# Norm factors of the delta-rule heads: four heads in one set of instructions

## The chip, the cores and the metric

The kernel runs on one core of one Trainium2 chip. The metric is the device time of one execution in microseconds (us); lower is better. Five engines work side by side, each through a queue of its own in order: TensorE (PE in the profile; its weight loads are PEld), VectorE (DVE), ScalarE (ACT), GpSimd (POOL), and SyncE (SP), which issues the DMAs here.

## The reference, cut to what matters

One layer of a decoder is computed for 1024 prompt tokens and 32 sample tokens: an input projection, two groups of heads side by side (four gated-delta heads of width 128, and sliding-window attention), an output projection, two layer norms and a SwiGLU. The change concerns the unit-length scaling of k and q in the delta heads:

```
def l2norm(t):
    return t * lax.rsqrt(jnp.sum(t * t, axis=-1, keepdims=True) + EPS)

q = l2norm(qc.reshape(Bn, L, H_A, DK_A)) * (DK_A ** -0.5)
k = l2norm(kc.reshape(Bn, L, H_A, DK_A))
...
A = jnp.where(strict, jnp.einsum('bnhid,bnhjd->bnhij', kb, kc) * decay, 0.0)      # kb = kc * beta
rhs = jnp.concatenate([vc * bc[..., None], kb * jnp.exp(gc)[..., None]], axis=-1)
...
o_n = q_dec S + qk v_new;   S = S * g_last + k_dec^T v_new
```

## The kernel before, in words

The prompt is taken in two passes, s = 0 (columns 0 to 511) and s = 1 (512 to 1055; its last 32 columns are the sample tokens). In each, 22 tiles of the input projection are multiplied one after the other; `conv_dense`, `kv_dense`, `q_dense` and `z_dense` issue them. Each weight quarter is split into a rounded part (`wh`, ACT, L162) and a remainder (`wl`, DVE, L163), and each product is three matmuls (L433 to L435). All other work is written as generators: `spawn` puts one on a list, and `pump` runs through the list between groups of matmuls until a budget of estimated work is spent. A generator that waits for a flag yields BLOCK and is passed over. `TileContext(nc, schedule_with_timeline_sim=True)` then lays out the order within each engine's queue from its own estimates, so neighbouring generators are interleaved.

The k and q of a head are not scaled by their norms; the scale is carried as factors, kept in the small tile `hs[s]` with fields of 4 x 4 columns (head x block of 128 tokens). In `delta_k(s, h)` ACT sums the squares of k (L668) into `ssk`; DVE adds EPS (L672), takes the reciprocal `rk2` (L673) and `wk` = rk2 times a decay (L674), and scales the block matrix `Ball` with rk2 (L678), which gives the flag K. Then it takes the reciprocal root of `ssk` in `rsqrt` (two integer instructions, L410 and L411, and three Newton steps of three instructions, L413 to L415) and from it `bsk` (L685, L686), flag B. `delta_q(s, h)` does the same for q (L806 to L816): `rq` and `rqe`, flag Q. So each head has a k chain and a q chain of 14 instructions of 128x4, each of which reads what the one before wrote.

Who reads them: `delta_v` scales v with `bsk` (L832) once B is set; `delta_w` waits for the inverse (flag E) and for Q; `recur` waits for Q, V and W of all heads and uses `wk` (L872), `rqe` (L887) and `rq` (L911, L914). `inverse(s)` waits for K of all heads and runs 31 steps of two instructions on POOL (L710, L712). At the same time DVE takes the row maxima of the attention scores (L1074, which frees the score banks in PSUM), the softmax scaling (L1096) and the convolutions (L642). `page` hands out a buffer of SBUF, and POOL clears its first column (L229) before anyone writes it; DVE's first writes of `pre` (L624, L626) wait for that.

Of the kernel before, what the change touches and what calls it, by code (L numbers as in the profile page):

```python
# [12 lines left out]
ALU = mybir.AluOpType  # L13
AX = mybir.AxisListType

P = 128
# [8 lines left out]
EPS = 1e-6  # L25
# [183 lines left out]
def _program(k):  # L209
# [3 lines left out]
    V, A, G = nc.vector, nc.scalar, nc.gpsimd  # L213
# [7 lines left out]
    def room(tag, n=1):  # L221
        return cap[tag] - live[tag] >= n
# [34 lines left out]
    def drop(tag="hp", n=1):  # L257
        live[tag] -= n
        assert live[tag] >= 0
# [13 lines left out]
    def b3(ap):  # L273

        return ap.unsqueeze(2).broadcast_to([P, 4, P])
# [6 lines left out]
    def spawn(g, quick=False):  # L282
        gens.append(g)
        if quick:
            fast.append(g)
# [17 lines left out]
    def need(cond):  # L303
        while not cond():
            assert pump(), "no progress"
# [5 lines left out]
    flags = set()  # L311

    def wait(*names):
        while not all(n in flags for n in names):
            yield BLOCK
# [92 lines left out]
    def rsqrt(x, y, a):  # L408

        V.tensor_scalar(a.bitcast(I32), x.bitcast(I32), 1, None, ALU.logical_shift_right)  # L410
        V.tensor_scalar(y.bitcast(I32), a.bitcast(I32), -1, 0x5F3759DF, ALU.mult, ALU.add)  # L411
        for _ in range(3):
            V.scalar_tensor_tensor(a, y, -0.5, y, ALU.mult, ALU.mult)  # L413
            V.tensor_tensor(a, a, x, ALU.mult)
            V.scalar_tensor_tensor(y, a, 1.5, y, ALU.add, ALU.mult)  # L415

    def groups(s):
        return [(0, 512)] if s == 0 else [(0, 272), (272, 272)]
# [53 lines left out]
    gat = {}  # L472
# [101 lines left out]
    hs = {}  # L574
# [45 lines left out]
    def conv_dense(s, ti, ft):  # L620
        need(lambda: room("hp", 2))
        pre = page([P, 3 + 512], F32, f"pre{s}{ft}")
        if s == 0:
            V.memset(pre[:, 0:3], 0.0)  # L624
        else:
            V.tensor_copy(pre[:, 0:3], carry[:, ft, :])  # L626

        def evac(ps, c0, cw):
            pw = min(512, c0 + cw) - c0
            A.copy(pre[:, 3 + c0:3 + c0 + pw], ps[:, :pw])  # L630
            if pw < cw:
                A.copy(XS[:, ft, :, 3:7], ps[:, pw:cw].rearrange("p (b t) -> p b t", t=4))

        dense(idx[f"in{s}"][TILES.index(ti)], *x_hl[s], evac, groups(s))
        return pre
# [14 lines left out]
    def delta_k(s, h, pre):  # L650

        F = hs[s]
        yield from have("hp", 2)
        kT = page([P, 512], F32, f"kT{s}{h}")
        kN = page([P, 4, P], F32, f"kN{s}{h}")
        heads[s, h] = d = {"kT": kT, "kN": kN}
        yield from conv(s, 4 + h, pre, kT)
        yield from have("ms", 2)
        pk, pb = bank(), bank()
        pk3 = pk.rearrange("p (n t) -> p n t", t=P)  # L660
        for n in range(4):
            tr(pk3[:, n, :], kT[:, n * P:(n + 1) * P], ident)
        for n in range(4):
            mm(pb[:, n * P:(n + 1) * P], kT[:, n * P:(n + 1) * P], kT[:, n * P:(n + 1) * P], start=True, stop=True)
        A.copy(kN, pk3)
        for n in range(4):
            jk = small([P, P], "junk", 1)
            A.activation(jk, pk3[:, n, :], AF.Square, accum_out=F["ssk"][:, h, n:n + 1])  # L668
        drop("ms")
        yield 1300.0  # L670
        ss, rk2, y, a = (F[n][:, h, :] for n in ("ssk", "rk2", "y", "a"))
        V.tensor_scalar(ss, ss, EPS, None, ALU.add)  # L672
        V.reciprocal(rk2, ss)  # L673
        V.tensor_tensor(F["wk"][:, h, :], rk2, gat[s]["ekd"][:, h * 4:h * 4 + 4], ALU.mult)  # L674
        yield from wait(("R", s, h))
        RB = Bm[s][:, h * 4:h * 4 + 4, :]
        for n in range(4):
            V.scalar_tensor_tensor(RB[:, n, :], pb[:, n * P:(n + 1) * P], rk2[:, n:n + 1], RB[:, n, :],  # L678
                                   ALU.mult, ALU.mult)
        drop("ms")  # L680
        flags.add(("K", s, h))
        yield 0.0
        rsqrt(ss, y, a)
        bsk = F["bsk"][:, h, :]
        V.tensor_tensor(bsk, ss, y, ALU.mult)  # L685
        V.tensor_tensor(bsk, bsk, gat[s]["beta"][:, h * 4:h * 4 + 4], ALU.mult)  # L686
        flags.add(("B", s, h))
        yield 0.0

    def inverse(s):  # L690
# [98 lines left out]
    def delta_q(s, h, pre):  # L789
        F = hs[s]  # L790
        yield from have("hp")
        qT = page([P, SG[s][1]], F32, f"mx{s}{h}")
        mixed[s, h] = qT
        yield from conv(s, h, pre, qT[:, 0:512])
        yield from wait(("R", s, h))
        yield from have("ms", 2)
        d = heads[s, h]
        R = Rt[s, h]
        pq, pb = bank(), bank()
        for n in range(4):  # L800
            tr(pq[:, n * P:(n + 1) * P], qT[:, n * P:(n + 1) * P], ident)
        for n in range(4):
            mm(pb[:, n * P:(n + 1) * P], d["kT"][:, n * P:(n + 1) * P], qT[:, n * P:(n + 1) * P], start=True, stop=True)
        for n in range(4):
            jk = small([P, P], "junk", 1)
            A.activation(jk, pq[:, n * P:(n + 1) * P], AF.Square, accum_out=F["ssq"][:, h, n:n + 1])  # L806
        for n in range(4):
            V.scalar_tensor_tensor(R[:, n, :], pb[:, n * P:(n + 1) * P], F["rk2"][:, h, n:n + 1], R[:, n, :],
                                   ALU.mult, ALU.mult)
        drop("ms", 2)  # L810
        yield 1300.0
        ss, rq, rqe, y, a = (F[n][:, h, :] for n in ("ssq", "rq", "rqe", "yq", "aq"))
        V.tensor_scalar(ss, ss, EPS, None, ALU.add)
        rsqrt(ss, y, a)
        V.tensor_scalar(rq, y, float(P) ** -0.5, None, ALU.mult)
        V.tensor_tensor(rqe, rq, gat[s]["eg"][:, h * 4:h * 4 + 4], ALU.mult)  # L816
        flags.add(("Q", s, h))
        yield 0.0

    def delta_v(s, h, pre):  # L820
        yield from have("hp", 2)
# [13 lines left out]
        yield 450.0  # L835

    def delta_w(s, h):
        yield from wait(("E", s), ("Q", s, h))
        yield from have("hp")
        d = heads[s, h]  # L840
        bE = page([P, 4, P], F32, f"bE{s}{h}")
        V.tensor_tensor(bE, Em[s][:, h * 4:h * 4 + 4, :], b3(gat[s]["bg"][:, h * 4:h * 4 + 4]), ALU.mult)
        yield 0.0
        yield from have("ms")
        pw = bank()
        for n in range(4):
            mm(pw[:, n * P:(n + 1) * P], d["kN"][:, n, :], bE[:, n, :], start=True, stop=True)
        drop()
        d["wT"] = d["kT"]
        A.activation(d["wT"], pw, AF.Copy, scale=-1.0)  # L850
        drop("ms")
        flags.add(("W", s, h))
        yield 900.0
# [3 lines left out]
    def recur(s):  # L857

        F, g = hs[s], gat[s]
        yield from wait(*[(x, s, h) for x in "QVW" for h in range(4)])  # L860
        hd = [heads[s, h] for h in range(4)]
        Eall = Em[s]
        if s:
# [1 line left out]
        for n in range(4):  # L865
# [42 lines left out]
            for h in range(4):  # L908
                o = hd[h]["vb"][:, n, :]
                rq = F["rq"][:, h, n:n + 1]  # L910
# [16 lines left out]
        v, y, a = F["oss"], F["y"], F["a"]  # L927
# [514 lines left out]
    def mix_in(s, before_last):  # L1442
        fields(s)
        pre = conv_dense(s, 0, 4)
        baT = ba_dense(s)
        if s == 0:
            params()
        spawn(gating(s, baT))
        for h in range(4):
            spawn(decay(s, h))  # L1450
        spawn(delta_k(s, 0, pre))
        for h in range(1, 4):
            spawn(delta_k(s, h, conv_dense(s, h, 4 + h)))
        spawn(inverse(s))
        spawn(keys(s, kv_dense(s, 12, "kb")))
        spawn(vals(s, kv_dense(s, 13, "vb")))
        for m in range(4):
            spawn(attn(s, m, q_dense(s, m)))
        if s:
            spawn(history())  # L1460
            spawn(sample_attn(), True)
        for h in range(4):
            spawn(delta_q(s, h, conv_dense(s, 4 + h, h)))
        for h in range(4):
            spawn(delta_v(s, h, conv_dense(s, 8 + h, 8 + h)))
            spawn(delta_w(s, h))
        spawn(recur(s))
        if s:
            spawn(sample_delta(), True)
        for h in range(3):  # L1470
            spawn(gate(s, h, z_dense(s, h)))
        hook = before_last()
        spawn(gate(s, 3, z_dense(s, 3, ktmajor=True, hook=hook)))
        if s == 0:
            spawn(spill())
        drop("xs", 8)
        hook(1)
# [179 lines left out]
    for f in range(NE):  # L1657
        q = quarters(f)
        plan[f] = {n: W.plain(W.raw(q[n])) for n in ("A11", "A12")}
    for f in range(NF):  # L1660
        q, early = quarters(f), f < NE
# [3 lines left out]
        p = plan.setdefault(f, {})  # L1665
# [36 lines left out]
    B = {}  # L1702
# [195 lines left out]
    for f in range(NF):  # L1898
        end = f == NF - 1
        p = plan[f]  # L1900
# [6 lines left out]
        q = banks("ms", HW_)  # L1907
# [13 lines left out]
        q = banks("acc", HW_)  # L1921
# [7 lines left out]
        q = banks("acc", 512)  # L1929
# [10 lines left out]
        q = banks("ms", HW_)  # L1940
# [151 lines left out]
```

## Time and profile before

| | |
|---|---|
| median of 3 runs | 1296.59 us (1295.82 to 1296.64) |
| profiled execution | 1296.37 us |
| its span, first to last instruction | 1294.6 us |
| granted TensorE clock over the span | 0.985 |
| busy: PE, PEld | 1253.7 us, 1130.8 us |
| busy: DVE, ACT, POOL | 889.3 us, 619.0 us, 396.1 us |

Times inside the profile count from the start of the span. An instruction's row gives its line in the kernel, its operation, and the tiles as out<-in; idle time in front of it stands in brackets with what ended it. The granted clock is a share of full speed: 1.00 is 2.4 GHz and 0.50 is 1.2 GHz, and a mean over a stretch lies between them.

### The profile page before, as it was taken

Reading aid. Unit: us, or ns where it says so; the run is one execution under the profiler, and the core shown is the slowest. Engines: PE = TensorE matmul, PEld = TensorE weight load, DVE = VectorE, ACT = ScalarE, POOL = GpSimd, SP = SyncE. Lnnn points to the kernel's source line nnn. Section 1 sums busy time; section 2 is a strip of 40 time slices with the busy share of each in tenths; the row PEclk is TensorE's granted clock in tenths of the full one; section 3 lists DMA queues with packets and bytes.
Section 4 is the critical chain, followed back from the end, with each engine's and each line's share of the span. In section 5 each row is a group of like instructions: output and inputs, shape, how many; then the busy total and the mean of one; then the engine's idle time right before and its main releaser. Section 6 shows DMA issues by size and latency. Waiting matters only on the chain.

```text
span 1294.6 us, 25112 instructions
## 1 busy us (share of the span) xinstructions
PE 1253.7 (97%) x8701; PEld 1130.8 (87%) x8701; DVE 889.3 (69%) x2041; ACT 619.0 (48%) x1376; POOL 396.1 (31%) x1207
## 2 busy tenths in 40 slices
PE   9998999999999999996999999999999999999996
PEld 7876789989889988985999999999999898788995
DVE  6797975888995679868866655555655775632664
ACT  7774754657656543586322222323324554522453
POOL 1008411203913134527643433222332112111210
PEclk9998999999899999998999999999999999999998
DMA  7422331242143556444544422222324886634461
GB/s 251 139 82 75 83 135 47 82 142 75 35 124 113 169 162 192 162 152 150 174 148 150 138 99 68 81 83 75 111 86 118 293 262 184 206 115 114 142 219 47
DMA packets 119103, 170.82 MB, mean 132 GB/s; under 512 B 20272, under 2 KB 50096, under 8 KB 118960
## 3 DMA queue, kind: packets, MB, share of 16 engines
q1 hardware_dynamic: 118976, 169.22, 41.7%
q8 instruction: 68, 1.11, 0.3%
q14 instruction: 59, 0.48, 0.1%
HBM read 138.44 MB, written 31.75 MB: 131 GB/s over the span
## 4 chain that ended last, share of the span: by engine, by line
PE 77%; DVE 12%; issue 3%; ACT 3%; DMA 2%; POOL 2%; DVEq 0%; SPq 0%; ACTq 0%; POOLq 0%
PE acc L1978 6%; PE acc L1807 6%; PE acc L1976 6%; PE acc L1977 6%; PE acc L1808 6%; PE acc L1809 6%; PE acc L433 5%; PE acc L434 5%; PE ms L1809 5%; PE ms L1807 5%; PE acc L435 5%; PE ms L1808 5%; DVE wl L163 2%; DVE st L1074 1%; PE ms L1123 1%
## 5 line engine op out<-in xcount | busy, mean ns | idle before, releaser
L163 DVE TENSOR_TENSOR wl<-wr,wh 128x512 fp32r<-128x512 f32 x330 | 238.6, 726 | 133.6 <-ACT wh L162 123.5
L162 ACT CAST wh<-wr 128x512 fp32r<-128x512 f32 x330 | 197.4, 602 | 264.1 <-PE acc L1977 104.9
L433 PE MATMUL acc<-xh,wh 128*128 128x272 f32 (+1 forms) x528 | 175.1, 332 | 0.2 <-DVE qs L1032 0.2
L435 PE MATMUL acc<-xh,wl 128*128 128x272 f32 (+1 forms) x528 | 173.9, 329 | 1.2 <-DVE wl L163 1.1
L434 PE MATMUL acc<-xl,wh 128*128 128x272 f32 (+1 forms) x528 | 173.6, 329 | 0.0
L1978 PE MATMUL acc<-hx,wl 128*128 128x272 f32 (+1 forms) x528 | 171.6, 325 | 1.9 <-DVE wl L163 1.8
L1976 PE MATMUL acc<-hx,wh 128*128 128x272 f32 (+1 forms) x528 | 171.9, 326 | 1.3 <-ACT wh L162 1.3
L162 ACT CAST wh<-S 128x512 fp32r<-128x512 f32 x88 | 54.4, 619 | 150.6 <-PE acc L1808 95.7
L1978 PEld LDWEIGHTS acc<-hx,wl 128*128 128x128 f32 x528 | 99.2, 188 | 11.4 <-DVE wl L163 3.2
L435 PEld LDWEIGHTS acc<-xh,wl 128*128 128x128 f32 x528 | 100.4, 190 | 9.2 <-DVE wl L163 1.8
L434 PEld LDWEIGHTS acc<-xl,wh 128*128 128x128 f32 x528 | 100.6, 190 | 8.5 <-issue 2.0
L433 PEld LDWEIGHTS acc<-xh,wh 128*128 128x128 f32 x528 | 100.5, 190 | 8.3 <-issue 1.0
L1976 PEld LDWEIGHTS acc<-hx,wh 128*128 128x128 f32 x528 | 99.1, 188 | 9.8 <-ACT wh L162 1.9
L1977 PE MATMUL acc<-hx,wh 128*128 128x272 f32 x352 | 101.4, 288 | 0.2 <-DVE hx L1706 0.2
L163 DVE TENSOR_TENSOR wl<-S,wh 128x512 fp32r<-128x512 f32 x88 | 72.1, 821 | 37.7 <-ACT wh L162 35.0
L1977 PE MATMUL acc<-hy,wh 128*128 128x512 f32 x176 | 69.2, 393 | 0.0
L1977 PEld LDWEIGHTS acc<-hx,wh 128*128 128x128 f32 x352 | 66.4, 189 | 0.7 <-DVE hx L1706 0.4
L433 PE MATMUL acc<-mh,wh 128*128 128x272 f32 (+1 forms) x192 | 64.0, 333 | 0.0
L434 PE MATMUL acc<-ml,wh 128*128 128x272 f32 (+1 forms) x192 | 63.4, 330 | 0.0
L435 PE MATMUL acc<-mh,wl 128*128 128x272 f32 (+1 forms) x192 | 63.0, 328 | 0.0
L1705 ACT CAST hx<-hr 128x272 fp32r<-128x272 f32 (+1 forms) x66 | 31.6, 485 | 47.4 <-DMA hr<-hd 43.1
L1647 POOL TENSOR_TENSOR S<-wr,S 128x512 f32<-128x512 f32 x22 | 34.7, 1577 | 54.5 <-DVE wl L163 54.5
(631 smaller groups left out, 3519.2 us busy)
## 6 DMA issues: line engine op xcount, KB each, us to landing
wr<-in_w_ffo_t SPq DMA_DIRECT2D x120, 256.0 KB, 3.0
wr<-in_w_ffi_t SPq DMA_DIRECT2D x108, 256.0 KB, 2.8
wr<-in_w_in_t SPq DMA_DIRECT2D x88, 256.0 KB, 2.8
wr<-in_w_out_t SPq DMA_DIRECT2D x32, 256.0 KB, 2.6
hd<-x SPq DMA_DIRECT2D x22, 272.0 KB, 2.5
hr<-hd SPq DMA_DIRECT2D x44, 136.0 KB, 2.7
hd<-x SPq DMA_DIRECT2D x22, 256.0 KB, 2.0
hr<-hd SPq DMA_DIRECT2D x22, 256.0 KB, 4.9
```

The costliest lines, as they stand in the source:

```text
L162: nc.scalar.copy(hi, raw)
L163: nc.vector.tensor_tensor(lo, raw, hi.bitcast(F32), ALU.subtract)
L433: mm(ps[:, :cw], wh, xh[kt][:, c0:c0 + cw], start=(kt == 0), stop=False)
L434: mm(ps[:, :cw], wh, xl[kt][:, c0:c0 + cw], start=False, stop=False)
L435: mm(ps[:, :cw], wl, xh[kt][:, c0:c0 + cw], start=False, stop=(kt == n - 1))
L1647: G.tensor_tensor(t["S2"], W.get(r["A12"]), t["S2"], ALU.subtract)
L1807: mm(o, wh[:, kt, :], xh, start=(start and kt == 0), stop=False, **kw)
L1808: mm(o, wh[:, kt, :], xl, start=False, stop=False, **kw)
L1809: mm(o, wl[:, kt, :], xh, start=False, stop=(kt == 3), **kw)
L1976: mm(ps, wh[:, f % 4, :], xh, start=(f == 0), stop=False)
L1977: mm(ps, wh[:, f % 4, :], xl, start=False, stop=False)
L1978: mm(ps, wl[:, f % 4, :], xh, start=False, stop=(f == NF - 1))
```

## The change

The k chain after the flag K, with `wk`, moves out of `delta_k` into a new generator `norms_k(s)`; the q chain moves out of `delta_q` into `norms_q(s)`. Each waits for all four heads and then works on the fields of all of them, 128x16 in place of 128x4. `norms_k` is spawned after the four `delta_k`, `norms_q` after the four `delta_q`. `delta_q` now sets a flag q as soon as its block matrix is scaled, for which `delta_w` waits; `recur` waits for one flag Q of the pass.

```
     def delta_k(s, h, pre):
...
-        ss, rk2, y, a = (F[n][:, h, :] for n in ("ssk", "rk2", "y", "a"))
+        ss, rk2 = (F[n][:, h, :] for n in ("ssk", "rk2"))
         V.tensor_scalar(ss, ss, EPS, None, ALU.add)
         V.reciprocal(rk2, ss)
-        V.tensor_tensor(F["wk"][:, h, :], rk2, gat[s]["ekd"][:, h * 4:h * 4 + 4], ALU.mult)
...
         flags.add(("K", s, h))
         yield 0.0
+
+    def norms_k(s):
+
+        yield from wait(*[("K", s, h) for h in range(4)])
+        ss, rk2, wk, bsk, y, a = (hs[s][n].rearrange("p h n -> p (h n)") for n in ("ssk", "rk2", "wk", "bsk", "y", "a"))
+        V.tensor_tensor(wk, rk2, gat[s]["ekd"][:, 0:16], ALU.mult)
         rsqrt(ss, y, a)
-        bsk = F["bsk"][:, h, :]
         V.tensor_tensor(bsk, ss, y, ALU.mult)
-        V.tensor_tensor(bsk, bsk, gat[s]["beta"][:, h * 4:h * 4 + 4], ALU.mult)
-        flags.add(("B", s, h))
+        V.tensor_tensor(bsk, bsk, gat[s]["beta"][:, 0:16], ALU.mult)
+        for h in range(4):
+            flags.add(("B", s, h))
+        yield 0.0
+
+    def norms_q(s):
+
+        yield from wait(*[("q", s, h) for h in range(4)])
+        ss, rq, rqe, y, a = (hs[s][n].rearrange("p h n -> p (h n)") for n in ("ssq", "rq", "rqe", "yq", "aq"))
+        V.tensor_scalar(ss, ss, EPS, None, ALU.add)
+        rsqrt(ss, y, a)
+        V.tensor_scalar(rq, y, float(P) ** -0.5, None, ALU.mult)
+        V.tensor_tensor(rqe, rq, gat[s]["eg"][:, 0:16], ALU.mult)
+        flags.add(("Q", s))
         yield 0.0
...
     def delta_q(s, h, pre):
...
         drop("ms", 2)
+        flags.add(("q", s, h))
         yield 1300.0
-        ss, rq, rqe, y, a = (F[n][:, h, :] for n in ("ssq", "rq", "rqe", "yq", "aq"))
-        V.tensor_scalar(ss, ss, EPS, None, ALU.add)
-        rsqrt(ss, y, a)
-        V.tensor_scalar(rq, y, float(P) ** -0.5, None, ALU.mult)
-        V.tensor_tensor(rqe, rq, gat[s]["eg"][:, h * 4:h * 4 + 4], ALU.mult)
-        flags.add(("Q", s, h))
-        yield 0.0
...
     def delta_w(s, h):
-        yield from wait(("E", s), ("Q", s, h))
+        yield from wait(("E", s), ("q", s, h))
...
     def recur(s):
-        yield from wait(*[(x, s, h) for x in "QVW" for h in range(4)])
+        yield from wait(("Q", s), *[(x, s, h) for x in "VW" for h in range(4)])
...
     def mix_in(s, before_last):
         for h in range(1, 4):
             spawn(delta_k(s, h, conv_dense(s, h, 4 + h)))
+        spawn(norms_k(s))
         spawn(inverse(s))
...
         for h in range(4):
             spawn(delta_q(s, h, conv_dense(s, 4 + h, h)))
+        spawn(norms_q(s))
```

## Rows read from the trace of the kernel before

**Rows 1.** The page, part 1: busy us (share of the span) and instructions of each engine.

```profile
PE 1253.7 (97%) x8701; PEld 1130.8 (87%) x8701; DVE 889.3 (69%) x2041; ACT 619.0 (48%) x1376; POOL 396.1 (31%) x1207
```

**Rows 2.** What the matrix engine waited for from 0 to 620 us: who, for whom, us in total, times, longest us.

```profile
PE ms L1070 <- DVE ast L1074: 5.0, 3, 4.2
...
PE ms L1070 <- DVE hs L415: 1.7, 1, 1.7
PE ms L982 <- ACT junk L668: 1.7, 1, 1.7
...
PE acc L435 <- DVE wl L163: 1.1, 1, 1.1
PE ms L1070 <- ACT mx L1127: 1.0, 1, 1.0
PE ms L563 <- ACT gt L554: 1.0, 1, 1.0
```

**Rows 3.** Busy time of each engine in stretches of 25 us (with the number of instructions), then the mean granted clock, the DMA share and GB/s.

```profile
125.00:150.00 25.00, 24.75 (x122) 20.65 (x123) 24.26 (x93) 19.79 (x70) 16.84 (x38) 0.90 0.21 55
...
250.00:275.00 25.00, 22.20 (x180) 21.56 (x179) 18.65 (x67) 17.55 (x60) 5.32 (x18) 1.00 0.59 176
...
325.00:350.00 25.00, 22.24 (x158) 21.86 (x157) 24.69 (x81) 14.66 (x41) 22.93 (x44) 0.86 0.10 32
```

**Rows 4.** Groups of DVE instructions from 0 to 480 us, shapes kept apart: count, busy us, mean ns of one, idle us before them.

```profile
L413 DVE SCALAR_TENSOR_TENSOR hs<-hs 128x4 f32<-128x4 f32 x48 | 9.7, 203 | 0.4
L415 DVE SCALAR_TENSOR_TENSOR hs<-hs 128x4 f32<-128x4 f32 x48 | 9.3, 196 | 0.4
...
L414 DVE TENSOR_TENSOR hs<-hs 128x4 f32<-128x4 f32 x48 | 8.3, 175 | 0.6
...
L410 DVE TENSOR_SCALAR hs<-hs 128x4 int32<-128x4 int32 x16 | 5.0, 312 | 0.0
...
L413 DVE SCALAR_TENSOR_TENSOR hs<-hs 128x16 f32<-128x16 f32 x6 | 1.0, 172 | 0.1
```

**Rows 5.** The same groups in two stretches: first 150 to 175 us, then 300 to 350 us.

```profile
L413 DVE SCALAR_TENSOR_TENSOR hs<-hs 128x4 f32<-128x4 f32 x6 | 0.9, 156 | 0.0
...
L413 DVE SCALAR_TENSOR_TENSOR hs<-hs 128x4 f32<-128x4 f32 x7 | 2.4, 339 | 0.1
```

**Rows 6.** DVE in order of time, first pass: start us, us, line, operation, tiles, shapes, count, idle time before it and what ended it.

```profile
102.76 0.16 DVE L686 TENSOR_TENSOR hs<-hs,gt 128x4 f32<-128x4 f32 x1
...
117.35 0.63 DVE L813 TENSOR_SCALAR hs<-hs 128x4 f32<-128x4 f32 x1
...
118.44 0.25 DVE L410 TENSOR_SCALAR hs<-hs 128x4 int32<-128x4 int32 x1
121.69 0.16 DVE L411 TENSOR_SCALAR hs<-hs 128x4 int32<-128x4 int32 x1 [3.00 <-issue]
121.71 0.06 DVE L624 MEMSET pre<- 128x3 f32 x1
...
122.60 1.10 DVE L163 TENSOR_TENSOR wl<-wr,wh 128x512 fp32r<-128x512 f32 x1
...
124.18 0.47 DVE L1074 CUSTOM_DVE_ANT_0 st<-ms,cst,par 128x256 f32<-128x256 f32 x1
```

**Rows 7.** DVE in order of time, second pass, 253 to 258 us.

```profile
253.65 1.22 DVE L410 TENSOR_SCALAR hs<-hs 128x4 int32<-128x4 int32 x1
...
257.39 0.19 DVE L551 COPY gt<-ms 128x34 f32<-128x34 f32 x1
```

**Rows 8.** DVE in order of time, second pass, 326 to 331 us.

```profile
326.47 0.60 DVE L813 TENSOR_SCALAR hs<-hs 128x4 f32<-128x4 f32 x1
...
327.64 0.57 DVE L410 TENSOR_SCALAR hs<-hs 128x4 int32<-128x4 int32 x1
...
329.93 0.52 DVE L414 TENSOR_TENSOR hs<-hs 128x4 f32<-128x4 f32 x1
330.37 0.47 DVE L1074 CUSTOM_DVE_ANT_0 st<-ms,cst,par 128x256 f32<-128x256 f32 x1
```

**Rows 9.** PE in order of time, the same place.

```profile
331.40 0.45 PE L1070 MATMUL ms<-kh,qs 128*128 128x128 f32 x1 [1.75 <-DVE hs L415]
```

**Rows 10.** What DVE waited for from 0 to 480 us: us in total, times, longest us.

```profile
DVE pre L626 <- POOL pre L229: 8.2, 2, 5.2
...
DVE pre L624 <- POOL pre L229: 5.1, 3, 3.7
```

**Rows 11.** Instructions that write or read the tile `hs`: count, ns min/median/max, first and last start in us, shapes.

```profile
L872 DVE TENSOR_SCALAR kd<-kN,hs x32: 268/281/558, 170.7 to 427.7; 128x128 f32<-128x128 f32 x32
...
L914 DVE SCALAR_TENSOR_TENSOR vb<-ms,hs,vb x28: 340/344/348, 212.2 to 453.5; 128x128 f32<-128x128 f32 x28
...
L686 DVE TENSOR_TENSOR hs<-hs,gt x8: 153/158/403, 33.8 to 322.1; 128x4 f32<-128x4 f32 x8
...
L816 DVE TENSOR_TENSOR hs<-hs,gt x8: 107/160/684, 132.2 to 370.9; 128x4 f32<-128x4 f32 x8
L832 DVE TENSOR_TENSOR vb<-ms,hs x8: 674/688/692, 182.3 to 401.6; 128x512 f32<-128x512 f32 x8
```

**Rows 12.** DVE in order of time, second pass: the first use of `bsk`.

```profile
395.48 0.69 DVE L832 TENSOR_TENSOR vb<-ms,hs 128x512 f32<-128x512 f32 x1 [5.60 <-PE ms L830]
```

**Rows 13.** Groups of POOL instructions from 306 to 360 us: count, busy us, mean ns of one, idle us before them.

```profile
L710 POOL TENSOR_TENSOR itmp<-Db,Ab 64x31 f32<-64x31 f32 (+15 forms) x31 | 18.9, 611 | 12.1 <-DMA Ab<-bd 10.3
```

## The prediction

> **What bounds the kernel now.** I read the page first, then the waits of the matrix engine, then busy time and granted clock by stretch, then the vector engine's groups and its order of work around each wait. The page gives the matrix engine (PE) 97% and the vector engine (DVE) 69% of the span [rows 1]: the kernel is bound by PE, and a cut on DVE is worth only what PE now waits for DVE, plus what such waits cost in clock. The norms lie in the two passes of the mixing stage, from about 30 us on (first tokens) and from 253 to 371 us (second) [rows 7, 11], so the wait list is asked for the front part of the span. The reader is to see there how short it is: PE waited for the DVE max of the attention scores (L1074) three times, 5.0 us in all and 4.2 at the longest; once for a norm instruction itself, 1.7; for the squares of the k heads on ACT, 1.7; for a weight split (L163), 1.1; for the gating exponentials (L554), 1.0; for a copy on ACT (L1127), 1.0 [rows 2]. To that comes clock. In 125 to 150 us the mean grant is 0.90, which is 2.5 us of full-speed work lost, and in 325 to 350 us it is 0.86, or 3.5 us; the drops, to the lower level of 1.2 GHz, follow the 4.2 us wait and the 1.7 us wait. Beside the other wait of 1.7, in 250 to 275, the grant stays 1.00 [rows 3]. So the ceiling of the change is near 11.5 us of waits plus 6.0 of clock.
>
> **What is removed.** Each of the four heads in each of two passes runs one chain of 14 small DVE instructions for k (11 of them the Newton root) and one of 14 for q: 224 instructions of 128x4. The k chain's first two, the add of EPS and the reciprocal (L672, L673), stay per head and are not among the 14. Afterwards four chains of 14 are left, 56 instructions of 128x16: 168 go. The main groups hold 160 of the 224 and take 9.7 + 8.3 + 9.3 + 5.0 = 32.3 us, 0.20 each [rows 4]. So 168 x 0.20 = about 34 us of instruction time go, as an upper bound, since neighbours overlap. The wide form is already in the trace, for the output norm: 172 ns against 156 for the narrow one in a quiet stretch [rows 4, 5]. The 56 wide ones thus add 56 x 0.016 = 0.9 us; I take the net as 33. Nothing is added to other engines, and no DMA is issued.
>
> **What of it PE sees.** Four places, each by the instructions that stand in DVE's queue ahead of what PE waited for. In all four it is a chain of an early head, which goes; only the fourth head's chain keeps its place.
>
> (a) Second pass, 331 us. The L1074 that frees the score bank starts at 330.37, and PE goes on at 331.40. From 327.64 to 330.37 DVE does nothing but the q chain of head 0, 2.7 us, with L813 before it [rows 8, 9]. Without the chain L1074 is more than 1.7 us earlier, so the wait of 1.7 goes, and with it, I expect, the clock's 3.5: a single wait of that length left the grant at 1.00 elsewhere [rows 3]. Term 5.2; lower bound 0, if other work is put into the gap; upper bound 6.2, with the wait for L1127.
>
> (b) First pass, 125 us. Ahead of L1074 at 124.18 stand L813, L410, then 3.0 us in which DVE did nothing until L411, then two more norm instructions around a split of 1.10 [rows 6]. If the pause belongs to L411, everything goes: 5.0 + 2.5 = 7.5. But the next instruction, L624, writes a page that POOL clears first, and it started 0.02 us after L411. DVE waited for such clears up to 3.7 and 5.2 us elsewhere [rows 10], so it may have stood there anyhow. Then only the norm instructions behind it go: 124.18 - 121.71 - 1.10 = 1.4. I take 1.4, as the neighbouring rows speak for POOL.
>
> (c) Second pass, 258 us. The copy of the gating sums (L551) runs at 257.39; the k chain of head 0 began with L410 at 253.65 and, with two splits, fills the time between [rows 7]. PE's wait for L554 behind it, 1.0, goes. The next wait, 1.7 for L668, hangs on the same gating data through a DMA and ACT's order: 0 to 1.7, taken as 0.
>
> (d) The wait for L163, 1.1, late in the second pass: the q chain of head 1 stands before it, but the merged q chain lands there too. 0 to 1.1, taken as 0.
>
> Sum: 5.2 + 1.4 + 1.0 = 7.6. All the rest of the 33 us is hidden under matmuls; if PE ever had no work there, it would be worth up to that.
>
> **What is moved.** bsk, wk and the q factors of heads 0 to 2 now come only after the fourth head. wk, bsk and rq are first read at 170.7, 182.3 and 212.2 us in the first pass; bsk at 395.5 in the second. The last k chains ended near 103 and 322, the last q chain at 371 [rows 6, 11, 12]: slack of over 20 us everywhere, so this costs nothing. The inverse waits for the K flags, which stay per head; delta_w may start earlier. In queues, DVE instructions alone are moved.
>
> **Under POOL.** While POOL runs the inverse, the same instruction takes 339 ns instead of 156 on the mean [rows 5], and single ones 0.60 to 0.63 [rows 6, 8], as long as one POOL instruction, 0.61 [rows 13]. The Trainium skill, "SBUF — State Buffer", Who interferes with whom, has the rule for it: a DVE instruction with two SBUF inputs and a GpSimd instruction that reads SBUF exclude each other, and the later one is blocked for the whole of the earlier. The trace agrees for single instructions and not for the mean. By that rule a chain of 14 could cost 14 x 0.61 = 8.5, and the kernel, if such a chain stood where (a) is, 1296.4 - 1.0 + 8.5 - 3.2 = 1300.7. By the mean of the row a chain of 14 costs 14 x 0.34 = 4.7 there.
>
> **Rivals.**
>
> Forecast: (a) and (c) go, (b) partly. 1296.4 - 7.6 = 1288.8. Chance 0.42, own range 1284 to 1293.
>
> All of it: (b) in full and (c), (d) at their upper bounds. 7.6 + 6.1 + 1.7 + 1.1 = 16.5, so 1279.9. For it speaks that all waits listed stand behind norm instructions; against, L624 and the ACT order. Chance 0.13.
>
> Hidden: PE is at 97%, and where DVE is freed it runs sooner into a page that POOL has not yet cleared (8.2 + 5.1 us of such waits [rows 10]). Then the order is re-laid and waits of the same size come back: 1294 to 1299, centre 1296.4. The Trainium skill, "Perfetto Trace Analysis", Identifying the Most-Contended Engine, says to work on the engine with the highest occupancy, which is not DVE here. Chance 0.25.
>
> The merged k chain takes the q chain's place, the slower side. It can start only after the fourth head; the fourth chain already ended as late as 322.1 [rows 11]. If it slips behind that, it stands ahead of L1074 as one run of 14 dependent instructions while POOL works. At 0.34 each it takes 4.7 instead of the q chain's 3.2: (a) is not gained and 1.5 is lost. At 0.60 each, which single rows show, 8.4, so 5.2 is lost: 1296.4 - 1.0 + 5.2 = 1300.6. It decides from about 3.2 + 1.0 + 2.6 = 6.8 us ahead of L1074. Against it: where the fourth k chain stands now, up to 322.1, no wait of the list is put down to it. Chance 0.20.
>
> **The numbers.** The profiled execution took 1296.37 us around its span of 1294.6; the median of the runs is 1296.59, so the sum holds for it within 0.2. Predicted 1289. The range runs from inside "all of it" to inside the slower case: 1281 to 1300. About 0.2%, 2.6 us, is what this measurement can tell from no change: faster (under 1294.0) 0.42 + 0.13 and a little of "hidden", 0.57; same 0.24; slower 0.19.
>
> **What would show it.** Right: 56 instructions of 128x16 with the root's lines beside the output norm's; DVE busy some 25 to 33 us lower, all before 375 us; no PE wait of 1.7 behind a norm instruction and a grant of 1.00 in the second pass's attention; PE's wait for L554 gone. (b) is right if PE's long wait in the first pass shrinks to about 2.8 and the grant still dips. Wrong if a new wait of several us behind L1074 or L163 appears in 96 to 144 or 311 to 356 us, where POOL runs, with a dip of the grant; or if the waits after 375 us, where nothing is changed, move by as much as the gain.

## The result, and the profile after

The changed kernel takes 1291.59 us (median of 8 runs, 1285.95 to 1294.52) against 1296.62 (1295.82 to 1298.24); the ratio is 0.9948, 95% interval 0.9935 to 0.996. The profiled execution took 1288.69 us around a span of 1286.8, so it is one of the faster of the eight.

First the page's busy time per engine:

```profile
PE 1248.8 (97%) x8701; PEld 1127.1 (88%) x8701; DVE 871.9 (68%) x1873; ACT 616.2 (48%) x1374; POOL 395.9 (31%) x1207
```

The 168 instructions are gone from DVE, and PE is busy 4.9 us less [rows 1]; it has the same matmuls, and most of the difference is less time at the lower clock (3.4 us of it before 405 us, see below). Next, the groups of DVE instructions from 0 to 480 us (count, busy us, mean ns of one, idle us before them):

```profile
L413 DVE SCALAR_TENSOR_TENSOR hs<-hs 128x16 f32<-128x16 f32 x18 | 3.4, 186 | 0.3
L415 DVE SCALAR_TENSOR_TENSOR hs<-hs 128x16 f32<-128x16 f32 x18 | 3.3, 184 | 0.3
L414 DVE TENSOR_TENSOR hs<-hs 128x16 f32<-128x16 f32 x18 | 3.2, 180 | 0.2
L410 DVE TENSOR_SCALAR hs<-hs 128x16 int32<-128x16 int32 x6 | 2.5, 409 | 0.0
```

The wide form costs as much as the narrow one [rows 4]: where there were 48 of 0.20 us there are 18 of 0.18, six of them the output norm's. (The mean of 409 ns for L410 comes of a single one of 1.30 us; the median is 0.17.) All instructions that write `hs` fell from 53.9 to 18.9 us by their durations summed. Then what PE waited for from 0 to 620 us (total, times, longest):

```profile
PE ms L1080 <- DVE ast L1084: 3.3, 3, 1.5
PE ms L992 <- ACT junk L668: 2.3, 1, 2.3
PE ms L754 <- DVE hs L699: 2.0, 1, 2.0
...
PE ms L563 <- ACT gt L554: 1.1, 1, 1.1
PE ms L1080 <- ACT junk L822: 1.1, 1, 1.1
```

and the stretches (busy us of PE, PEld, DVE, ACT, POOL; then granted clock, DMA share, GB/s):

```profile
125.00:150.00 25.00, 23.64 (x120) 19.00 (x118) 23.80 (x69) 22.40 (x78) 16.83 (x38) 1.00 0.30 83
250.00:275.00 25.00, 21.66 (x165) 21.18 (x163) 16.03 (x41) 15.84 (x51) 1.07 (x7) 0.93 0.46 147
325.00:350.00 25.00, 24.07 (x195) 23.52 (x194) 21.48 (x65) 19.99 (x66) 22.12 (x46) 1.00 0.14 43
350.00:375.00 25.00, 23.05 (x343) 21.59 (x342) 22.07 (x50) 11.56 (x32) 3.04 (x12) 0.93 0.48 135
```

Line numbers are shifted: L1070 and L1074 are now L1080 and L1084, L982 is L992, the inverse's first matmul L738 is L754. The row maximum, 5.0 us of waits with one of 4.2, is down to 3.3 with none over 1.5, and the grant is 1.00 in 125 to 150 and in 325 to 350 us, where it was 0.90 and 0.86 [rows 2, 3]. But the wait for L668 has grown from 1.7 to 2.3, and there is a new one of 2.0 for the inverse, each with a stretch at the lower level (0.93). DVE and PE in order of time at the second:

```profile
355.26 0.70 DVE L746 STREAM_TRANSPOSE Dl<-Eall 32x512 f32<-32x512 f32 x1 [0.63 <-DMA Eall<-ed]
355.90 0.12 DVE L699 TENSOR_SCALAR hs<-hs 128x16 f32<-128x16 f32 x1
```

```profile
356.02 0.24 PE L754 MATMUL ms<-Dl,Ball 32*32 32x32 f32 x2 [1.95 <-DVE hs L699]
```

The row names L699, the first instruction of the merged q chain, but the transpose of the inverse's result, which the matmul reads, ended only 0.06 us before it, at 355.96.

**Where the 5 us arise.** The order of the projection matmuls is known, so one can ask how much earlier each starts than the same one (by count) in the kernel before. At the end of the first pass (232 us) it is 3.66 us, at the end of the mixing stage's second input pass (405 us) 5.41. (Between these points the figure also holds matmuls of other work that stand earlier or later in PE's queue.) From there to 1004 us it drifts to 5.85, and it ends at 7.7: the last 1.9 come in a stage in which nothing was changed, and lie in waits that this execution happens not to have. So 5.4 is the change's part, close to the 5.0 of the medians. It can be accounted for: up to 405 us PE's idle time fell from 13.6 to 11.7, and what it lost at half clock from 6.8 to 3.4 (half of the time spent at the 0.50 grant); together 5.3.

This is one execution of each kernel. Over the whole span the profiled pair differs by 4.5 us of full-speed work lost to the clock. The mean grants of the other executions are nearer to each other: 0.9885 in the eight of the changed kernel and 0.987 in 104 of the kernel before from the rounds below (one of 0.938 left out; the profiled one had 0.985), which is about 2 us. So on the mean the clock's part of the 5 us is smaller than in this pair.

### The profile page after: what moved, and what is told of

Read it like the earlier page. It is cut to its first block, busy times and chain, and to the rows that moved or that the text cites. A ratio compares the mean times of both kernels' runs of the same rounds, so it can differ in the third digit from the quotient of the medians.

```text
span 1286.8 us, 24943 instructions
## 1 busy us (share of the span) xinstructions
PE 1248.8 (97%) x8701; PEld 1127.1 (88%) x8701; DVE 871.9 (68%) x1873; ACT 616.2 (48%) x1374; POOL 395.9 (31%) x1207
## 4 chain that ended last, share of the span: by engine, by line
PE 48%; DVE 2%; DMA 1%; ACT 0%; issue 0%; DVEq 0%; SPq 0%; ACTq 0%; POOL 0%; POOLq 0%
PE acc L1990 6%; PE acc L1988 6%; PE acc L1989 6%; PE acc L1821 5%; PE acc L1819 5%; PE acc L1820 5%; PE ms L1819 5%; PE ms L1821 5%; PE ms L1820 5%; DMA hr<-hd 1%; DVE y L1554 1%; DVE wl L163 0%; PE ms L1522 0%; DMA wr<-in_w_ffo_t 0%; PE ms L1497 0%
## 5 line engine op out<-in xcount | busy, mean ns | idle before, releaser
L163 DVE TENSOR_TENSOR wl<-wr,wh 128x512 fp32r<-128x512 f32 x330 | 238.1, 725 | 141.0 <-ACT wh L162 131.6
L163 DVE TENSOR_TENSOR wl<-S,wh 128x512 fp32r<-128x512 f32 x88 | 72.2, 823 | 37.7 <-ACT wh L162 34.9
```

The costliest lines, as they stand in the source:

```text
L163: nc.vector.tensor_tensor(lo, raw, hi.bitcast(F32), ALU.subtract)
```

## The experiments

Twelve kernels were run. In the table, "saved" is the lead over the kernel before at 232 and at 405 us, "idle" PE's idle time from 5 to 405 us, and "clock" half of the time at half clock there, all from one profiled execution each. "PE rows moved" counts the matrix instructions that stand elsewhere in PE's queue than in the kernel it was made from, as the planner laid it out; of `k_only` and the changed kernel, than in the kernel before. The traces hold no such listing; by the line and the tiles of each matmul in the traces, 12 places differ in `moved_only`, 4 in `before_nocl`, 134 in `q_only`, 172 in `q_nocl` and 480 to 1310 in the others.

| kernel | ratio to before (95%) | PE rows moved | saved at 232, at 405 | idle | clock |
|---|---|---|---|---|---|
| before | 1 | | 0, 0 | 13.6 | 6.8 |
| changed | 0.9948 (0.9935 to 0.996) | 917 | 3.7, 5.4 | 11.7 | 3.4 |
| q_only | 1.0003 (0.9991 to 1.0015) | 94 | 0.3, 0.6 | 15.2 | 5.1 |
| k_only | 0.9958 (0.9942 to 0.9973) | 916 | 3.0, 3.8 | 14.3 | 1.7 |
| moved_only | 1.0003 (0.9992 to 1.0015) | 10 (of before) | 0.3, 1.7 | 14.6 | 3.4 |
| no_steps | 0.9983 (0.9969 to 0.9998) | 572 | 2.8, 1.7 | 14.0 | 5.1 |
| before_r1 | 1.0007 (0.9993 to 1.0022) | 680 | 0.1, -1.2 | 15.7 | 6.8 |
| before_r4 | 0.9999 (0.9986 to 1.0012) | 569 | -0.5, -1.3 | 16.4 | 3.4 |
| after_r1 | 0.998 (0.9968 to 0.9991) | 698 | -0.3, -0.8 | 13.1 | 6.8 |
| after_r4 | 0.9932 (0.9912 to 0.9952) | 336 | 2.6, 5.1 | 12.9 | 1.7 |
| before_nocl | 1.0005 (0.9994 to 1.0016) | 4 | 1.3, -5.0 | 19.8 | 6.8 |
| q_nocl | 1.0022 (1.0008 to 1.0036) | 119 (of before_nocl) | -1.4, -4.3 | 18.5 | 8.5 |
| after_nocl | 0.9976 (0.996 to 0.9992) | 388 | 0.7, 0.0 | 14.7 | 6.8 |
| after_half | 0.9981 (0.9971 to 0.9991) | 771 | 6.5, 4.1 | 11.5 | 5.1 |

In every row idle plus clock differs from the 20.5 of the kernel before by what was saved at 405, within 2.2 us. All have the same 8701 matmuls, so whatever moved the time did it through these two. Single executions of a kernel differ by several us, though, and the profiled one of `moved_only` is the fastest of its 12, that of `after_nocl` the slowest: differences of 1 or 2 us in these columns show little.

**One half of the change at a time: q_only, k_only.** `q_only` has `norms_q` of the diff and leaves `delta_k` as it was. `k_only` has `norms_k` and gives each q head its own chain, but ahead of the pause (`yield 1300.0`) behind which the kernel before has it.

```
 q_only:   +spawn(norms_q(s))      delta_k with its own chain of 14, no norms_k
 k_only:   +spawn(norms_k(s))      delta_q with its own chain of 14, ahead of yield 1300.0, no norms_q
```

> The norms of q alone are taken for all four heads at once; those of k stay per head as before. 84 of the 168 instructions go, and the order of the other engines' work hardly changes. Theory 1 (what counts is which instructions stand in the vector engine's queue ahead of the max that frees a score bank; in both passes that is the q chain of head 0): the wait of 4.2 us near 125 us shrinks by 1.4 us or more, the wait of 1.7 near 331 us goes with its dip of the clock, and the time is 1290 to 1292, as with the whole change. Theory 2 (the work of the mixing stage is laid out anew and the gain is that of another layout): no gain, 1295 to 1298, as the layout stays. Theory 3 (each instruction less is worth the same, wherever it stood): half of the 5 us, about 1294.

> The norms of k alone are taken for all four heads at once; those of q stay per head as before. 84 of the 168 instructions go. Theory 1 (the q chain ahead of the bank-freeing max): no gain, 1295 to 1298, and the wait near 331 us with its half clock is still there. Theory 2 (another layout): a change of some us to either side, with waits at new places. Theory 3 (each instruction the same): about 1294.

It came out the other way round: q alone is worth nothing, 1.0003, and the kernel with the k norms merged and the q chains left per head has 0.9958, with an interval that overlaps the changed kernel's. Theory 1, which is the forecast's own, is wrong for q, and so is theory 3; theory 2, another layout, is left, and further runs test it. For k the test is not clean: with the pause behind it, the q chain of head 0 begins at 322.09 us in `k_only` instead of 326.47 [rows 8], so more than the k norms was changed. PE waits 1.8 us there, at 332.25, behind a clear of POOL's, and its clock does not fall.

Why q fails is plain in its trace. What PE waited for from 5 to 480 us in `q_only`:

```profile
PE ms L1075 <- DVE ast L1079: 7.4, 3, 3.7
```

The wait behind L415 near 331 us is gone as forecast, and at 330 us `q_only` is 3.0 us ahead. But the row maximum now costs 7.4 us. DVE in order of time, first pass and second pass:

```profile
117.86 0.08 DVE L1079 DVE_READ_ACCUMULATOR2_ANT ast<- 128x1 f32 x1
121.69 0.06 DVE L624 MEMSET pre<- 128x3 f32 x1 [3.75 <-POOL ptS L229]
...
333.51 0.08 DVE L1079 DVE_READ_ACCUMULATOR2_ANT ast<- 128x1 f32 x1
337.29 0.17 DVE L626 COPY pre<-carry 128x3 f32<-128x3 f32 x1 [3.71 <-POOL ptS L229]
...
338.43 0.47 DVE L1079 CUSTOM_DVE_ANT_0 st<-ms,cst,par 128x256 f32<-128x256 f32 x1
```

and PE behind it:

```profile
339.46 0.55 PE L1075 MATMUL ms<-kh,qs 128*128 128x256 f32 x1 [3.52 <-DVE ast L1079]
```

DVE, freed of the q chain, runs into the next clear of a `pre` page, 3.7 us too early, and PE waits 3.5 with 6.8 us at half clock: at 350 us `q_only` is 1.6 us behind. POOL reaches that clear when it always did. POOL in order of time in the kernel before, at the two places,

```profile
121.55 0.09 POOL L229 MEMSET pre<- 128x1 f32 x1
...
337.15 0.09 POOL L229 MEMSET pre<- 128x1 f32 x1
```

in `q_only`

```profile
121.53 0.09 POOL L229 MEMSET pre<- 128x1 f32 x1
...
337.17 0.09 POOL L229 MEMSET pre<- 128x1 f32 x1
```

and in the changed kernel

```profile
116.62 0.09 POOL L229 MEMSET pre<- 128x1 f32 x1
...
330.97 0.09 POOL L229 MEMSET pre<- 128x1 f32 x1
```

Here lies what differs with the k norms merged. The clears stand in POOL's queue between the 62 instructions of the inverse. In the changed kernel the inverse starts at 97.14 us instead of 98.44 (in `k_only` 96.65), and the clear of the first pass stands behind 28 of its instructions instead of 31: it comes 4.9 us earlier in all. In the second pass the inverse starts at 305.51 instead of 311.54 (in `k_only` 309.61). POOL in order of time before and after the change:

```profile
311.54 0.23 POOL L710 TENSOR_TENSOR itmp<-Db,Ab 64x31 f32<-64x31 f32 x1 [10.25 <-DMA Ab<-bd]
```

```profile
305.51 0.23 POOL L726 TENSOR_TENSOR itmp<-Db,Ab 64x31 f32<-64x31 f32 x1 [1.83 <-DMA Ab<-bd]
```

DVE still waits for the clears in the changed kernel,

```profile
116.77 0.06 DVE L624 MEMSET pre<- 128x3 f32 x1 [3.38 <-POOL pre L229]
...
331.10 0.17 DVE L626 COPY pre<-carry 128x3 f32<-128x3 f32 x1 [2.23 <-POOL ptS L229]
```

but PE waits 1.5 at the most behind them. The first of these clears comes 4.9 us earlier, with PE 0.5 us ahead (at 100 us); the second 6.2 us earlier, about as much as PE is ahead there (6.4 us at 330), while in `q_only` it stood still against a lead of 3.0.

**The place and the number apart: moved_only, no_steps.** `moved_only` has both chains at their new places, but each as a loop over the heads; `no_steps` is the kernel before with `rsqrt` cut down to its two integer instructions in the k and q chains, so that the three Newton steps are left out.

```
 moved_only, norms_k:  for h in range(4): wk, rsqrt, bsk on [:, h, :]     (norms_q likewise)
 no_steps:             rsqrt(ss, y, a)  ->  seed(ss, y, a)                (L410, L411 alone)
```

> Both chains stand where the change puts them, after the fourth head, but each is four chains of 128x4 one behind the other: the 224 narrow instructions of before at the merged places, none removed. Theory 1 (the place ahead of the max, not the number): 1290 to 1293, the waits near 125 and 331 us shrunk or gone; the longer runs of narrow instructions (56 in a row, 4 x 2.7 us and more) may cost up to 2 us near 362 us. Theory 2 (another layout): some us to either side. Theory 3 (the number of instructions): no gain, 1295 to 1298.

> The kernel before with the three Newton steps of the k and q roots left out (the first guess is used as it stands): each chain has 5 instructions instead of 14, at its old place, so 144 of 224 go. Theory 1: the q chain of head 0 ahead of the max is 9/14 of 2.7 us shorter, 1.7 us, as much as the wait near 331 us, so that this wait and its dip of the clock go: 1290 to 1293. Theory 2 (another layout): some us to either side, with waits at new places. Theory 3 (144/168 of the 5 us): about 1292.

The place alone is worth nothing (1.0003); PE's queue differs from that of before in 10 rows, and the first-pass clear comes 31 instructions into the inverse, as before. Fewer instructions at the old places, in another layout, give 0.9983: 2.8 us in the first pass (its longest wait there is 2.3, with no half clock), of which 1.1 are given back in the second. Its inverse starts later in the first pass (101.85 us instead of 98.44), and the clear comes only 0.8 us earlier (120.75).

**The layout by itself: before_r1, before_r4, after_r1, after_r4.** The planner lays all queues out anew when its estimates change, so a part of the result may be luck of the layout.

```
 r1:  V.reciprocal(rk2, ss)          r4:  delta_q:  yield 1300.0
     +yield 0.0                                  -> yield 900.0
```

> The kernel before with one more point, behind the reciprocal of a k head, at which the program may turn to other work; no instruction is added or taken away. This alone lays the order of some 700 matrix instructions of the mixing stage anew. If the 5 us of the change are those of another layout, the time moves by 2 to 6 us to one side or the other (waits and half-clock stretches at new places). If they are those of the k norms' fewer instructions, it stays at 1295 to 1299.

> The kernel before with the weight of a q head at the place where it pauses cut from 1300 to 900; no instruction is added or taken away, and some 570 matrix instructions stand elsewhere. Layout: 2 to 6 us to one side or the other. Fewer instructions: 1295 to 1299.

> The changed kernel with the same extra point at which the program may turn to other work; some 700 matrix instructions stand elsewhere, none is added or taken away. Layout: the gain of 5 us may be lost or doubled, anywhere in 1287 to 1300. Fewer instructions: 1290 to 1293, 5 us below the kernel before with the same point.

> The changed kernel with the weight of a q head at the place where it pauses cut from 1300 to 900; some 340 matrix instructions stand elsewhere, none is added or taken away. Layout: anywhere in 1287 to 1300. Fewer instructions: 1290 to 1293, 5 us below the kernel before with the same weight.

Two new layouts of the kernel before stay within 0.1% of it. The same two of the changed kernel give 0.998 and 0.9932. So merging the k norms gains in each of the four layouts tried without other edits (`k_only`, the changed kernel and its two variants), but between 0.2 and 0.7%, and layouts without it gain nothing. Against the kernel before with the same edit the medians differ by 3.0 us in r1 and by 9.0 in r4, so that neither is the 5 that "fewer instructions" expected.

The clears and the inverse go with this. The first-pass clear (the one at 121.55 in the kernel before) comes at 115.1 to 116.9 us in all four, and at 119.8 to 122.0 in the kernel before, its two variants, `q_only`, `moved_only` and `no_steps`. The second-pass inverse starts at 305.5, 307.5 and 309.6 in three of the four; in the fourth, `after_r1`, which gains least, it starts at 312.0, and in the kernels without the merge at 310.7 to 311.9.

In `after_r1` the clock takes the gain: PE reaches the inverse's matmul too early in the first pass (its row names no releaser; the transpose that it reads ended at 149.09). PE in order of time, and the stretch behind it:

```profile
149.19 0.22 PE L755 MATMUL ms<-Dl,Ball 32*32 32x32 f32 x2 [1.65 <-issue]
```

```profile
150.00:160.00 10.00, 9.18 (x98) 6.79 (x99) 9.64 (x27) 3.47 (x6) 0.47 (x6) 0.66 0.20 68
```

The grant of 0.66 over 10 us is 3.4 us of lost work, and with the wait that is about what the kernel had gained: it is 3.9 us ahead at 148 us and 0.3 behind at 232.

**The clears themselves: before_nocl, after_nocl, q_nocl.**

```
-        G.memset(t[:, 0:1].bitcast(F32), 0.0)
+        if clear:
+            G.memset(t[:, 0:1].bitcast(F32), 0.0)
...
+        pre = page([P, 3 + 512], F32, f"pre{s}{ft}", clear=False)
```

> The kernel before; only the one-column clear that POOL writes into each page of the convolution's input is left out (24 such clears; the page is written in full afterwards anyhow, its first three columns by the vector engine). The order on the other engines stays nearly as it was (4 matrix instructions move). Theory A (the vector engine stood still at 118.7 to 121.7 us for such a clear, which was queued on POOL behind 31 steps of the inverse, and PE's wait of 4.2 with its half clock came of that; the change gained the first pass by getting this clear earlier): the wait near 125 us shrinks to 1.5 or less, its half clock goes, 3 to 6 us are gained, 1290 to 1294. Theory B (the gain came of the fewer k instructions as such): no gain, 1295 to 1299.

> The changed kernel without POOL's clears of the convolution's input pages. Theory A: the first-pass part of the gain is the same time as in the kernel before without these clears, so that it adds little to the change: 0 to 3 us below the changed kernel, 1288 to 1292, and 5 us of difference between before and changed shrink to 1 to 3. Theory B: the difference between before and changed stays at 5 us with the clears gone from both.

> The norms of q alone taken at once, and POOL's clears of the convolution's input pages left out. With the clears there, taking the q chain away from ahead of the max at 331 us removed the wait of 1.7 but the vector engine then stood 3.7 us for the clear that POOL came to at 337.2, and PE waited 3.5 with half clock. Theory A: without the clears this second wait doesn't come, and the q norms are worth their 1.7 to 5 us: that much below the kernel before without the clears. Theory B: they are worth nothing again, equal to the kernel before without the clears within 1.5 us.

The first half of theory A holds. DVE in order of time in `before_nocl`, to be read beside [rows 6] (lines are one higher):

```profile
118.59 0.24 DVE L411 TENSOR_SCALAR hs<-hs 128x4 int32<-128x4 int32 x1
118.61 0.06 DVE L625 MEMSET pre<- 128x3 f32 x1
118.86 0.17 DVE L412 TENSOR_SCALAR hs<-hs 128x4 int32<-128x4 int32 x1
```

The pause of 3.0 us is gone, so it was the clear's; PE's wait shrinks from 4.2 to 1.2 and no half clock follows. The second half fails: nothing is gained, 1.0005. DVE and PE later in the same kernel:

```profile
363.72 0.70 DVE L731 STREAM_TRANSPOSE Dl<-Eall 32x512 f32<-32x512 f32 x1 [3.70 <-DMA Eall<-ed]
```

```profile
364.47 0.31 PE L739 MATMUL ms<-Dl,Ball 32*32 32x32 f32 x2 [4.16 <-DVE hs L411]
```

PE is 5.7 us ahead at 350 us and 5.0 behind at 405: it waits for the inverse, 4.2 us and 10.2 us at half clock. (L411, which the row names, ended 0.05 us after the transpose.) With the q norms merged as well it waits 4.9 in the first pass and 7.4 in the second, and the kernel is slower, 1.0022, which fits neither theory: by the medians it stands 2.9 us above `before_nocl`. In `after_nocl` the waits for the inverse are 4.3 and 3.4. At 0.9976 it is worse than the changed kernel, against theory A, and 3.5 us below `before_nocl`, between the 1 to 3 of A and the 5 of B.

**A shorter inverse: after_half.** The 64 systems are spread over 128 partitions.

```
-        Ab = bigt([64, 32, 32], "Ab");  Db = bigt([64, 32, 32], "Db")
+        Ab = bigt([P, 32, 32], "Ab");   Db = bigt([P, 16, 32], "Db")      # partition 64*u + p: columns 2*j + u
...
+            nr, ns = 31 - c, c // 2 + 1
+            G.tensor_tensor(tv, bc(Db[:, 0:ns, c:c + 1], [P, ns, nr]), bc(Ab[:, c:c + 1, c + 1:], [P, ns, nr]), ALU.mult)
```

> The changed kernel with the inverse spread over 128 partitions instead of 64: each of the 64 triangular systems is split over two partitions, even columns on one and odd ones on the other, so that an instruction of a step handles up to 136 elements per partition instead of 256, at the price of two more transfers. By the instructions of the trace (0.25 us at 31 elements, 0.64 at 256) the 62 instructions take some 10 us less per pass. Theory A (the time out of the mixing stage follows the end of the inverse on POOL: 356.2 us in the kernel before, 349.1 in the changed one, and with POOL's clears gone PE waited for it next): the inverse ends 8 us or more earlier in both passes, PE's waits for it (1.95 us with half clock near 356 us) and part of those behind POOL's clears go, 3 to 7 us below the changed kernel, ratio to the kernel before 0.989 to 0.993. Theory B (the gain came of the vector engine's fewer k instructions, and the earlier end of the inverse is only its sign): as the changed kernel within 1.5 us, ratio 0.994 to 0.996, with waits of the same size elsewhere.

POOL's groups from 90 to 150 us in `after_half` (count, busy us, mean ns of one, idle us):

```profile
L730 POOL TENSOR_TENSOR Db<-Db,itmp 128x126 f32<-128x126 f32 (+22 forms) x31 | 13.9, 450 | 2.0
L728 POOL TENSOR_TENSOR itmp<-Db,Ab 128x126 f32<-128x126 f32 (+22 forms) x31 | 13.4, 433 | 6.6 <-DMA Ab<-bd 4.5
```

The inverse ends at 129.2 and 338.6 us instead of 143.0 and 349.1, and the first pass gains: 6.5 us saved instead of 3.7. The second gives it back. PE in order of time there:

```profile
349.54 0.21 PE L757 MATMUL ms<-Dl,Ball 32*32 32x32 f32 x1 [2.91 <-DVE R L827]
```

PE now starts the inverse's matmul 6.5 us earlier (349.54 instead of 356.02) and has waited 2.9 for it again: the result came back through DRAM only at 344.5 (DVE stood 3.5 us for `Eall<-ed`), the last of DVE's three transposes ended at 348.34, and L827, which the row names, follows it on DVE. The ratio is 0.9981, worse than the changed kernel; theory A fails, and so does B, by which nothing should have moved. No version beat the changed kernel clearly; `after_r4`, 0.9932, has an interval that overlaps with its own.

## Why the prediction was right, and where not

The forecast was 1289, in a range of 1281 to 1300 that would have held no change as well; 1291.59 came, 5.0 us gained instead of 7.6. That it came so near is in part luck. By the leads above the first pass gave 3.7 us where 1.4 was forecast, and the second 1.8 (5.4 less 3.7) where 6.2 was. Of the four terms one came for a reason that was only half of it, one was too small, and two were wrong.

**(a), 5.2 us at 331 us.** The wait and the half clock are gone in the changed kernel, as foreseen, and between 300 and 330 us the lead grows from 2.1 to 6.4. But the cause given, the q chain ahead of the maximum, is not enough. `q_only` takes the q chains alone away from there, and is 0.6 us ahead at 405. The step that failed is the one that asks what is late next: the prediction had DVE running into uncleared pages among its rivals, as "hidden", but did not look for the clear that follows 331 us. It comes at 337.15, and in the changed kernel, with the earlier inverse, at 330.97. (Another layout can move it, too: in `before_r1` it comes at 333.37, though the inverse starts when it did.)

**(b), 1.4 us at 125 us.** Putting the 3.0 us pause down to POOL's clear was right, as `before_nocl` and `q_only` show. The size was wrong: 3.7 us were saved in the first pass, of which 3.4 are the half clock. The prediction took the clear's time as fixed; it came 4.9 us earlier.

**(c), 1.0 us for the gating sums.** Wrong: PE's wait for L554 is 1.07, where it was 1.0. The next wait, for L668, rose from 1.7 to 2.3 and now has 3.4 us at half clock behind it, though the prediction took it as 0 because the grant had stayed at 1.00 there.

**(d), taken as 0.** The wait of 1.1 for L163 is gone; in its place stands 1.95 for the inverse at 356.02, with a stretch at half clock.

**Moved parts.** That `bsk`, `wk` and the q factors come later cost nothing, as said. "The inverse waits for the K flags, which stay per head" is the sentence in which the gain was missed: the last head's `Ball` was scaled at 297.1 us instead of 301.4, and the inverse followed.

**Under POOL.** The merged k chain of the second pass ran from 297.0 to 315.1, interleaved with other work and not as one run, and eight of its 14 instructions stood before POOL began the inverse (305.51). Of its twelve instructions from L411 on, the six before that took 0.12 to 0.17 us, the six after it 0.16 to 0.56, 0.31 on the mean. The Trainium skill, "SBUF — State Buffer", Who interferes with whom, has a DVE instruction with two SBUF inputs contend with a GpSimd instruction that reads SBUF, for ports that one of them holds exclusively. The trace agrees in that the slower ones stand under the inverse, and 0.56 is nearly a whole POOL instruction (0.61); most took less. The slower rival, a chain in one run ahead of the maximum, did not occur.

**The signs named.** DVE's busy time fell by 17.4 us, not 25 to 33: the durations of the removed work sum to 35.0, but records of neighbours overlap, and other DVE instructions up to 480 us took 405.2 instead of 392.8 us summed. The grant of 1.00 in the second pass's attention came as written, and so did the absence of a new wait of several us behind the maximum; the 2.0 put down to L699, a norm instruction, is the inverse's. PE's wait for L554 did not go. In the first pass the long wait shrank to 1.5, not to 2.8, and the grant does not dip, so by its own sign (b) was not right.

**Still open.** Whether the k norms gain because DVE has less to do, or because the planner, with fewer of them to place, finds a layout in which the inverse starts earlier. Each k-merged kernel changes both; `moved_only` keeps the old layout and gains nothing, two other layouts of the old kernel gain nothing, but two are few. `no_steps`, with 72 k instructions fewer at the old places and no earlier inverse, speaks against the first, but its layout is another one as well. Open too is what the k norms do alone, since `k_only` moves the q chains. A kernel with the k norms merged in the old queue order would tell both; it wasn't tried.

## What to carry to other kernels

Where an engine with slack is relieved, don't stop at the wait that goes: follow that engine to its next wait for a third one (here the page clears, queued on POOL between the steps of a long side chain) and that chain to the matmul that needs it. Do the halves of a change apart before believing the place that the profile points to. And where a planner orders the queues, run the edit in two or three neutral layouts: here one edit gave 0.2 to 0.7%.

## What the runs showed that was not expected

A pause can stand in front of the wrong instruction. In [rows 6] 3.00 us without a releaser stand ahead of L411, while the instruction behind it, L624, shows no wait; without the clear that L624 waits for, the pause ahead of L411 is gone, and in `q_only`, which has no L411 there, a pause of 3.75 that ends at the same time stands ahead of L624.

The same idle time on PE can go with a stretch at the lower clock or without one. PE in order of time behind the wait for L668, first in the changed kernel, where the lower level (0.50) was granted for 3.4 us from 264.2 on, then in `q_only`, where the grant stayed at 1.00:

```profile
263.27 0.33 PE L992 MATMUL ms<-cst,kb 128*128 128x128 f32 x1 [2.27 <-ACT junk L668]
```

```profile
271.51 0.33 PE L987 MATMUL ms<-cst,kb 128*128 128x128 f32 x1 [2.33 <-ACT junk L668]
```

The wait of 4.2 near 125 us had 6.8 us at half clock with it in the kernel before, and 3.4 in `moved_only`. Over the kernels of the table the half clock cost 1.7 to 8.5 us in the input passes, about as much in range as the idle time (11.5 to 19.8) does: it is a term of its own in a sum.

On POOL, twice the partitions with about half the elements on each took 0.44 to 0.46 us per instruction, on the mean of a pass, instead of 0.62 to 0.66.
